# Mixer gates grouped by function over both halves, earlier load of x's second half, other column pacing and another end in a four-layer decoder trunk

## Chip, cores and metric

The kernel runs on one core of a Trainium2 chip. The metric is the device time of one execution in microseconds. Three runs of the kernel before took 1739.61, 1742.8 and 1742.51 us, median 1742.51.

## What is computed

x is (1024 positions, 1024 features), c one vector of 1024. Two blocks, each a token mixer and a squared-ReLU MLP, every one of the form x + gate(c) * f(RMSNorm(x) * (1 + scale(c)) + shift(c)), then a last RMSNorm. All values are float32. The reference, cut to what the change touches:

```python
cond = silu(c)
for i in range(2):
    mod = cond @ w_mod[i] + b_mod[i]                 # 6 x 1024 columns
    sh_m, sc_m, gt_m, sh_f, sc_f, gt_f = split(mod, 6)
    h = rms_norm(x, norm_mix_g[i]) * (1 + sc_m) + sh_m
    y = recurrent_mixer(h) if i == 0 else pool_mixer(h)
    x = x + gt_m * y
    h = rms_norm(x, norm_ffn_g[i]) * (1 + sc_f) + sh_f
    x = x + gt_f * (relu(h @ w1[i]) ** 2 @ w2[i])
return rms_norm(x, final_norm_g)

# recurrent_mixer
g = gelu(h @ w_y + b_y)
u = causal_conv4(h @ w_in + b_in)                    # width 4, per channel
r = sigmoid(u @ w_a + b_a); i = sigmoid(u @ w_x + b_x)   # 4 heads of 256 x 256
log_a = 8 * r * log_sigmoid(lam); a = exp(log_a)
s = scan: s_t = a_t * s_{t-1} + sqrt(1 - exp(2 log_a)) * i * u
return (s * g) @ w_out + b_out
```

## The kernel before

Features lie on the 128 partitions in 8 blocks, positions on the free axis in two halves of 512 (`x[0]`, `x[1]`). Every matrix product is split: a value v is kept as a high part of the TensorE type and a low rest, and `mm3` (L184) does three products, high by high, high by low, low by high, of 128x128 weights by 128x512. `proj` (L192) is 24 such products into one accumulator. There are 6 accumulators (`ps_mm`, L53), so a product group starts only when an earlier group was read out. Weights come as 512 KB units: `split_unit` (L168) loads one through SP's DMA queue into one of 3 raw buffers, copies the high part on ACT (L180) and subtracts the low part on DVE (L181), or on POOL, or with an accumulating DMA ("dma").

The modulation columns: `mod_column` (L205) is one DVE pass over a 512 KB piece of w_mod (`mb`, 128x1024) that multiplies by cond and sums. The first layer's scale and shift go another way (below); the other 10 vectors have 8 pieces each, 80 in all, in the order (0,2) (0,4) (0,3) (0,5) and then layer 1's. `drip(n)` (L229) does the next n of them; `split_unit` drips `rate[0]` or a given number after each load, `drip_until` (L233) does what is missing when a vector is needed. A piece takes one of the same 3 raw buffers and stands in DVE's order like any instruction.

The start: SP's queue gets vec, x's first half, and then in the order of the string at L113 the w_mod pieces `mw` 0 to 7 (digits; scale piece j=1, then shift piece j=0) and the four parts of the first projection's weights ("w"). `load_x(1)`, x's second half, comes at L409 behind two units of w_in. The loop at L380 does the first projection for half 0 (`ps6`, 18 products a block, L401) while scale and shift are still being computed. Its order on ACT, DVE and POOL is fixed by `after` (L321), which puts each instruction behind the one before on its engine: on DVE `bias_of(k)`, `scale_of(k+1)`, `hl` of block k, `normed(k+3)`. Squares of x's second half and their sums (`s1`, L443) follow behind the loop, then the copies `xr` that empty `ps6` (L426), two more projections, the scale `bc1` by the sums, the convolution (L431; four taps on ACT and DVE) and half 1.

The gates (L502) run per head and half: split of the head's input `xchl` (L507, L508), 8 groups of products of 6 products for two halves (4 per call), sigmoid of each, Exp and Tanh, a square on POOL (L529) and a multiply on DVE (L530), Sqrt (L533), products and the scan (L537). Behind each call two `gelu_block` (L542), each one `proj`, a gelu on ACT (L545) and a multiply on DVE. sigmoid, Exp and Tanh, Sqrt, and gelu need four different tables on ACT, and a load stands before each change. `split_y` (L550) splits the result for the output projection.

Elsewhere the order on each engine is made by a planner that takes the code's order as priority and its own estimate of when inputs are ready; `tc.issue_after` pins what is written in it.

After the output projection (L586, 8 drips in its first part), `ffn_norm` (L571) and 16 chunks of MLP follow (`f1`, `f2_fast`, `f2`), and the pooling mixer between them. `f1(0, 0)` (L858) has `ffn_norm(0, 1)` behind its first block, so PE does L272, the sums of x's half 1, there. `DRIPS` (L680) is one column for every unit of a chunk.

The end: `last_chunk` (L1013) does the last MLP product for half 0, for the first 256 positions of half 1 and for the rest. `SumSq` (L244) squares each new block of x on ACT and adds on DVE ("V") or opens a second part ("X"). The last norm uses `rstd_row` (L993), which sums over partitions with a 128x128 matrix of ones into 128x256 and takes root and reciprocal of that; the others use `rstd_bcast` (L265), which sums into 128x2 (one column per 128 positions), takes root and reciprocal there, and spreads with two more products.

Of the kernel before, what the change touches and what calls it, by code (L numbers as in the profile page):

```python
# [42 lines left out]
def trunk_kernel(ctx, tc, xT, vecs, wmod, w_k, w_in, w_y, w_g, w_out, w_p, w1, w2, outT):  # L43
# [69 lines left out]
    for what in "0ww1w2w34567":  # L113
        if what == "w":
            q = len(k_raw)
            if q == 0:
                kr = slot("kr")
            r2 = kr[:, q, :]
            r1 = slot("kr3", (D,)) if q == 3 else rawp.tile([P, D + 256], F32, tag="raw", name=f"raw_k{q}")[:, 0:D]
            k_raw.append((r1, r2))  # L120
            for part in range(2 if q == 0 else 1):
                for r, c0 in ((r1, 0), (r2, D)):
                    lo, hi = piece(r, q, part)
                    nc.sync.dma_start(r[:, lo:hi], w_k[q, :, c0 + lo:c0 + hi])
        else:
            e = int(what)
            for j in (1, 0):
                mod_raw[j, e] = mw[e][:, j, :]
                nc.sync.dma_start(mod_raw[j, e], wmod[0, j, e])
# [114 lines left out]
    class SumSq:  # L244


        def __init__(self, name, n=H, plan="GGGGGGGG", room=None):
            self.name, self.n, self.plan, self.room = name, n, plan, room
            self.parts = {}
            self.i = 0  # L250

# [12 lines left out]

    def rstd_bcast(ss, trace=None):  # L265
# [3 lines left out]
        ps = small_ps()  # L269
        for q in range(nq):  # L270
            for pi, a in enumerate(parts):
                PE.matmul(out=ps[:, q:q + 1], lhsT=a[:, q * P:(q + 1) * P], rhs=ones[:, 0:1],  # L272
                          start=(pi == 0), stop=(pi == len(parts) - 1))
# [99 lines left out]

    low = prepare(0)
# [5 lines left out]
    for k in range(NB):  # L380
# [15 lines left out]
        if k + 3 < NB:  # L396
            normed(k + 3)
        for low, r in ((0, hh), (0, hl), (1, hh)):
# [10 lines left out]
    load_x(1)  # L409
# [33 lines left out]
    s1 = SumSq("m01", plan="VVVVVVVV")  # L443
    for k in range(NB):
        s1.add(x[1][:, k, :])
# [56 lines left out]
    def gates(hd, unit, h):  # L502

        xchl = slot("xchl", (2, 2, H), F32R)
        xch, xcl = xchl[:, 0, :, :], xchl[:, 1, :, :]
        src = xc[h][:, 2 * hd:2 * hd + 2, :]
        S.copy(xch, src)  # L507
        V.tensor_sub(xcl, src, xch.bitcast(F32))  # L508
        rs, gs = [], []
        for mi in range(2):  # L510
            b = 2 * hd + mi
            for g in range(2):
                ps = acc_mm()
                for k in range(2):
                    mm3(ps, unit, ((g * 2 + k) * 2 + mi) * P, xch[:, k, :], xcl[:, k, :], k == 0, k == 1)
                t = tmp("gate")
                S.activation(t, ps, AF.Sigmoid, bias=vcol("ba" if g == 0 else "bx", b))
                (rs if g == 0 else gs).append(t)
        aa = []
        for mi in range(2):  # L520
            b = 2 * hd + mi

            av = tmp("a")
            S.activation(av, rs[mi], AF.Exp, scale=coef[:, b:b + 1])
            S.activation(rs[mi], rs[mi], AF.Tanh, scale=ncoef[:, b:b + 1])
            aa.append(av)
        for mi in range(2):
            e = tmp("asq")
            G.tensor_mul(e, aa[mi], aa[mi])  # L529
            V.scalar_tensor_tensor(rs[mi], e, 1.0, rs[mi], op0=ALU.add, op1=ALU.mult)  # L530
        for mi in range(2):
            b = 2 * hd + mi
            S.activation(rs[mi], rs[mi], AF.Sqrt)  # L533
            hs = xc[h][:, b, :]
            G.tensor_mul(gs[mi], gs[mi], hs)
            V.tensor_mul(gs[mi], gs[mi], rs[mi])
            V.tensor_tensor_scan(hs, aa[mi], gs[mi], 0.0 if h == 0 else carry[:, b:b + 1],  # L537
                                 op0=ALU.mult, op1=ALU.add)
            if h == 0:
                V.tensor_copy(carry[:, b:b + 1], hs[:, H - 1:H])  # L540
# [141 lines left out]
    def f1_jobs(i, c, eng=None):  # L682
        return [partial(lambda j: split_unit(w1[i, c * 4 + j], f"w1_{i}_{c}_{j}", eng, DRIPS[j]), j) for j in range(4)]
# [309 lines left out]
    def rstd_row(ss):  # L993

        parts = list(ss.parts.values())
        ps = small_ps()[:, 0:ss.n]
        for pi, a in enumerate(parts):
            PE.matmul(out=ps, lhsT=ones, rhs=a, start=(pi == 0), stop=(pi == len(parts) - 1))
        r = tmp("rrow", ss.n)
        S.activation(r, ps, AF.Sqrt, bias=eps, scale=1.0 / D)  # L1000
        V.reciprocal(r, r)
        return r

# [9 lines left out]
    def last_chunk(h, t0, n, plan, side=iter(())):  # L1013
        s = SumSq(f"o{h}{t0}", n, plan)
# [22 lines left out]
    sc = last_chunk(1, n1, H - n1, "VVVVVVVX", mid_norm())  # L1037
    final_norm(rstd_row(sc), 1, n1, H - n1)
# [71 lines left out]
```

## Time and profile before

| | us |
|---|---|
| median of 3 runs | 1742.51 |
| profiled execution | 1740.37 |
| its span, first to last instruction | 1738.5 |
| PE busy | 1690.5 (97%) |
| DVE busy | 1358.9 (78%) |
| ACT busy | 967.2 (56%) |
| POOL busy | 492.3 (28%) |
| DMA, mean | 108 GB/s; 340 GB/s in the first 60 us |

The profile is one execution. Times are in us from the span's start; PE is the TensorE matmul, PEld its weight load, DVE VectorE, ACT ScalarE, POOL GpSimd, SPq SyncE's DMA queue. In a timeline row the number in brackets is the engine's idle time before the instruction and who ended it. PE's mean granted clock is 0.994 of full.

The stages: first projection 0 to 58, the rest of w_in and the convolution to about 122, gates and gelu to about 250, output projection to about 359, then MLP and pooling, the last norm from 1700.

### The profile page before, as it was taken

The page shows a single profiled execution, that of the slowest core. Times are in us where ns is not written, and L with a number is a line of the kernel's source. Part 1 is how long each engine was busy: PE and PEld are TensorE (multiplying, and loading weights), DVE is VectorE, ACT ScalarE, POOL GpSimd, SP SyncE. Part 2 cuts the span into 40 slices and gives each one's busy share as a digit, 9 for nine tenths or more (in the row PEclk, how much of TensorE's full clock was granted, in tenths as well). Part 3 has the DMA queues.
Part 4 walks back from the last instruction along what each step waited for, and adds up shares of the span by engine and source line. Part 5 has one row for each costly group of instructions (what it writes and reads, how often), then busy time and mean ns, then how long its engine had stood idle before and what let it go on. Part 6 is the DMA issues. An engine that isn't in the chain of part 4 may idle for free.

```text
span 1738.5 us, 20871 instructions
## 1 busy us (share of the span) xinstructions
PE 1690.5 (97%) x7472; PEld 1386.7 (80%) x7472; DVE 1358.9 (78%) x2115; ACT 967.2 (56%) x1660; POOL 492.3 (28%) x419
## 2 busy tenths in 40 slices
PE   6899999999999999999999999999999999999997
PEld 4687778877788888888888888888878787878787
DVE  7897867589898989897973898559696868687847
ACT  6588886555454454545457787745444454545432
POOL 2132343103241414151416333303140405041403
PEclk9999999999999999999999999999999999999999
DMA  9423425642423333332319888841111112120202
GB/s 337 168 93 104 143 85 162 143 119 83 136 72 123 95 99 109 96 117 89 123 37 198 202 192 179 190 118 61 49 59 39 61 38 70 39 69 29 80 6 97
DMA packets 63175, 187.33 MB, mean 108 GB/s; under 512 B 6752, under 2 KB 9184, under 8 KB 63072
## 3 DMA queue, kind: packets, MB, share of 16 engines
q1 hardware_dynamic: 47376, 157.43, 27.6%
q0 software_dynamic: 15696, 28.58, 9.9%
q8 instruction: 58, 0.95, 0.2%
q14 instruction: 45, 0.37, 0.1%
HBM read 181.79 MB, written 4.19 MB: 107 GB/s over the span
## 4 chain that ended last, share of the span: by engine, by line
PE 75%; DVE 10%; issue 3%; ACT 3%; DMA 2%; POOL 1%; DVEq 0%; ACTq 0%; POOLq 0%
PE mm L188 25%; PE mm L189 25%; PE mm L190 25%; DMA mb<-in_wmod 2%; DVE mb L207 1%; DVE xa L773 1%; DVE xb L773 1%; POOL xa L782 1%; DVE xcb L440 1%; DVE w_a_s L181 1%; ACT c L777 0%; DVE gate L530 0%; PE sm L272 0%; DVE w_y L181 0%; DVE w_s L181 0%
## 5 line engine op out<-in xcount | busy, mean ns | idle before, releaser
L188 PE MATMUL mm<-hh,w_w 128*128 128x512 f32 x1024 | 399.7, 390 | 0.9 <-DVE xa L773 0.9
L189 PE MATMUL mm<-hl,w_w 128*128 128x512 f32 x1024 | 399.3, 390 | 0.0
L190 PE MATMUL mm<-hh,w_w 128*128 128x512 f32 x1024 | 399.0, 390 | 0.0
L782 POOL TENSOR_TENSOR xb<-xb,c 128x512 f32<-128x512 f32 x104 | 150.0, 1442 | 625.4 <-ACT c L777 625.2
L188 PEld LDWEIGHTS mm<-hh,w_w 128*128 128x128 f32 x1024 | 192.6, 188 | 43.1 <-DVE xa L773 3.0
L190 PEld LDWEIGHTS mm<-hh,w_w 128*128 128x128 f32 x1024 | 192.6, 188 | 40.2
L189 PEld LDWEIGHTS mm<-hl,w_w 128*128 128x128 f32 x1024 | 192.5, 188 | 39.5
L782 POOL TENSOR_TENSOR xa<-xa,c 128x512 f32<-128x512 f32 x104 | 159.7, 1535 | 145.2 <-ACT c L777 145.2
L777 ACT ACTIVATE c<-c,mod 128x512 f32<-128x512 f32 x104 | 75.3, 724 | 202.6 <-DVE c L803 135.5
L623 ACT ACTIVATE relu<-mm 128x512 f32<-128x512 f32 x128 | 76.2, 596 | 144.7 <-PE mm L190 144.7
L207 DVE SCALAR_TENSOR_TENSOR mb<-mb,cond 128x1024 f32<-128x1024 f32 x80 | 114.5, 1434 | 47.9 <-DMA mb<-in_wmod 47.9
L773 DVE SCALAR_TENSOR_TENSOR xa<-mm,mod,xa 128x512 f32<-128x512 f32 x156 | 113.0, 742 | 25.8 <-POOL xa L782 25.8
L181 DVE TENSOR_TENSOR w_w<-raw_w,w_w 128x512 fp32r<-128x512 f32 x112 | 106.8, 962 | 12.4 <-ACT w_w L180 12.4
L165 POOL DMA_DIRECT2D w_w<-in_w x80 | 70.5, 900 | 151.0 <-ACT w_w L164 120.6
L613 DVE TENSOR_TENSOR u<-usq,u 128x512 fp32r<-128x512 f32 x102 | 70.2, 688 | 16.1 <-ACT u L612 15.8
L188 PE MATMUL mm<-u,w_a_a 128*128 128x512 f32 x200 | 79.1, 396 | 2.3 <-DVE xb L773 1.2
L188 PE MATMUL mm<-u,w_w 128*128 128x512 f32 (+1 forms) x224 | 80.9, 361 | 0.0
L189 PE MATMUL mm<-u,w_w 128*128 128x512 f32 (+1 forms) x224 | 80.5, 360 | 0.1
L190 PE MATMUL mm<-u,w_w 128*128 128x512 f32 (+1 forms) x224 | 80.4, 359 | 0.0
L180 ACT CAST w_w<-raw_w 128x512 fp32r<-128x512 f32 x112 | 65.1, 612 | 25.0 <-PE mm L190 17.3
L189 PE MATMUL mm<-u,w_a_a 128*128 128x512 f32 x200 | 78.0, 390 | 0.0
L190 PE MATMUL mm<-u,w_a_a 128*128 128x512 f32 x200 | 77.9, 389 | 0.0
(326 smaller groups left out, 4030.0 us busy)
## 6 DMA issues: line engine op xcount, KB each, us to landing
raw_w<-in_w SPq DMA_DIRECT2D x148, 512.0 KB, 3.5
mb<-in_wmod SPq DMA_DIRECT2D x80, 512.0 KB, 3.8
w_w<-in_w POOLq DMA_DIRECT2D x80, 256.0 KB, 5.5
mw<-in_wmod SPq DMA_DIRECT2D x16, 512.0 KB, 11.0
raw_in<-in_w_in SPq DMA_DIRECT2D x8, 512.0 KB, 7.0
raw_y<-in_w_y SPq DMA_DIRECT2D x8, 512.0 KB, 3.7
raw_o<-in_w_out SPq DMA_DIRECT2D x8, 512.0 KB, 4.2
outT<-o SPq DMA_DIRECT2D x12, 256.0 KB, 2.2
```

What stands on the lines that cost most here:

```text
L165: nc.gpsimd.dma_start(w[:, 1, 0:n], src, accum_op=ALU.add)
L180: S.copy(w[:, 0, 0:n], raw)
L181: (eng or V).tensor_sub(w[:, 1, 0:n], raw, w[:, 0, 0:n].bitcast(F32))
L188: PE.matmul(out=ps, lhsT=wh, rhs=rh, start=first, stop=False)
L189: PE.matmul(out=ps, lhsT=wh, rhs=rl, start=False, stop=False)
L190: PE.matmul(out=ps, lhsT=w[:, 1, c:c + P], rhs=rh, start=False, stop=last)
L207: V.scalar_tensor_tensor(raw, raw, 1.0, cond, op0=ALU.mult, op1=ALU.mult, accum_out=m[:, e:e + 1])
L613: eng.tensor_sub(u[n][:, 1, jj, :], src, u[n][:, 0, jj, :].bitcast(F32))
L623: S.activation(r, ps, AF.Relu)
L773: V.scalar_tensor_tensor(xb, ps, g[:, r + 4 * row:r + 4 * row + 1], xb, op0=ALU.mult, op1=ALU.add)
L777: S.activation(t, src, AF.Identity, scale=g[:, r + 4 * row:r + 4 * row + 1])
L782: G.tensor_add(xb, xb, t)
```

## The change

Four places. x's second half is loaded between the w_mod pieces 5 and 6 (`345x67`), and its squares are done in the hand-ordered loop, three behind block 5, three behind 6, two behind 7 (`square1`). `gates` takes both halves: all sigmoids of both, then the split of the next head's inputs for both, then POOL's product of gate and input, Exp and Tanh of all four, the squares, the Sqrt; Exp writes over the convolution's output, and half 0's gates have a slot of their own. The four gelu blocks of a head follow, and `split_y(0)` stands behind the last head. The drip rate per unit is 0, 2, 3, 3 for the heads' units in place of 0, 1, 2, 3, and the first w1 units drip none. The last norm's sum is made on PE, one group of column sums for the first five blocks and one for each of the last three, and `rstd_bcast` replaces `rstd_row`.

```diff
-    for what in "0ww1w2w34567":
+    for what in "0ww1w2w345x67":
...
+        elif what == "x":
+            load_x(1)
...
+    class LastSumSq(SumSq):
+        def add(self, xb):
+            if self.i == 0:
+                self.ps = small_ps()
+            if self.plan[self.i] == "V":
+                super().add(xb)
+                if "V" in self.plan[self.i:]:
+                    return
+                a = self.parts["V"]
+            else:
+                a = tmp("sq", self.n)
+                self.i += 1
+                S.activation(a, xb, AF.Square)
+            for q in range(self.n // P):
+                PE.matmul(out=self.ps[:, q:q + 1], lhsT=a[:, q * P:(q + 1) * P], rhs=ones[:, 0:1],
+                          start=(a is self.parts["V"] and q == 0), stop=(self.i == NB), skip_group_check=True)
...
-        ps = small_ps()
...
+        ps = ss.ps
+        if ps is None:
+            ps = small_ps()
...
+    s1 = SumSq("m01")
+    def square1(k):
+        sq = tmp("sq")
+        after(S.activation, sq, x[1][:, k, :], AF.Square)
+        a = s1.parts.setdefault("V", sq)
+        if a is not sq:
+            after(V.tensor_add, a, a, sq)
...
+        for k1 in {5: (0, 1, 2), 6: (3, 4, 5), 7: (6, 7)}.get(k, ()):
+            square1(k1)
...
-    load_x(1)
...
-    s1 = SumSq("m01", plan="VVVVVVVV")
-    for k in range(NB):
-        s1.add(x[1][:, k, :])
...
-    def gates(hd, unit, h):
+    def gates(hd, unit, halves):
...
+        rs, gs = {}, {}
+        for h in halves:
+            xchl = split.pop((hd, h)) if (hd, h) in split else split_gate(hd, h)
+            room = slot("gates") if h == 0 else None
+            for mi in range(2):
+                b = 2 * hd + mi
+                for g in range(2):
+                    ps = acc_mm()
...
+                    t = tmp("gate") if room is None else room[:, 2 * mi + g, :]
+                    S.activation(t, ps, AF.Sigmoid, bias=vcol("ba" if g == 0 else "bx", b))
+                    (rs if g == 0 else gs)[h, mi] = t
+        if hd < 3:
+            for h in halves:
+                split[hd + 1, h] = split_gate(hd + 1, h)
+        both = [(h, mi) for h in halves for mi in range(2)]
+        hs = {(h, mi): xc[h][:, 2 * hd + mi, :] for h, mi in both}
+        for at in both:
+            G.tensor_mul(gs[at], gs[at], hs[at])
+        for at in both:
+            b = 2 * hd + at[1]
+            S.activation(hs[at], rs[at], AF.Exp, scale=coef[:, b:b + 1])
+            S.activation(rs[at], rs[at], AF.Tanh, scale=ncoef[:, b:b + 1])
+        for at in both:
             e = tmp("asq")
+            G.tensor_mul(e, hs[at], hs[at])
+            V.scalar_tensor_tensor(rs[at], e, 1.0, rs[at], op0=ALU.add, op1=ALU.mult)
+        for at in both:
+            h, b = at[0], 2 * hd + at[1]
+            S.activation(rs[at], rs[at], AF.Sqrt)
+            V.tensor_mul(gs[at], gs[at], rs[at])
+            V.tensor_tensor_scan(hs[at], hs[at], gs[at], 0.0 if h == 0 else carry[:, b:b + 1],
                                  op0=ALU.mult, op1=ALU.add)
...
-        rate[0] = hd
+        rate[0] = (0, 2, 3, 3)[hd]
...
+        gates(hd, ug, (0, 1))
         for h in range(2):
-            gates(hd, ug, h)
-            if (hd, h) == (3, 1):
-                split_y(0)
             for mi in range(2):
                 gelu_block(2 * hd + mi, uy[mi], h)
+    split_y(0)
...
-        return [partial(lambda j: split_unit(w1[i, c * 4 + j], f"w1_{i}_{c}_{j}", eng, DRIPS[j]), j) for j in range(4)]
+        return [partial(lambda j: split_unit(w1[i, c * 4 + j], f"w1_{i}_{c}_{j}", eng, 0 if (i, c) == (0, 0) else DRIPS[j]), j) for j in range(4)]
...
-    sc = last_chunk(1, n1, H - n1, "VVVVVVVX", mid_norm())
-    final_norm(rstd_row(sc), 1, n1, H - n1)
+    sc = last_chunk(1, n1, H - n1, "VVVVVXXX", mid_norm())
+    final_norm(rstd_bcast(sc), 1, n1, H - n1)
```

## Rows read from the trace of the kernel before

**Rows 1.** The page, busy time: engine, us, share of the span, instructions.
```profile
PE 1690.5 (97%) x7472; PEld 1386.7 (80%) x7472; DVE 1358.9 (78%) x2115; ACT 967.2 (56%) x1660; POOL 492.3 (28%) x419
```

**Rows 2.** PE's waits, whole span: line, releaser, us in total, times, longest.
```profile
PE mm L188 <- ACT gelu L545: 6.1, 4, 1.9
PE mm L188 <- ACT xr L426: 4.0, 1, 4.0
...
PE sm L272 <- DVE mod L210: 3.9, 1, 3.9
```

**Rows 3.** Timeline 42 to 79: start, us, engine, line, operation, idle before.
```profile
42.23 1.34 DVE L328 CUSTOM_DVE_ANT_0 mw<-mw,cond,bmix 128x1024 f32<-128x1024 f32 x1
42.35 0.81 ACT L328 ACTIVATE hh<-xn,mod,amix 128x512 fp32r<-128x512 f32 x1 [2.57 <-DVE mod L328]
...
46.75 1.07 PE L401 MATMUL mm<-hl,w_k 128*128 128x512 f32 x4
...
55.97 0.63 ACT L258 ACTIVATE ssqm01V<-xb 128x512 f32<-128x512 f32 x1 [1.42 <-DMA xb<-in_xT]
...
59.58 2.28 DVE L263 TENSOR_TENSOR ssqm01V<-ssqm01V,sq 128x512 f32<-128x512 f32 x3
...
61.11 3.56 ACT L426 ACTIVATE xr<-mm,vec 128x512 f32<-128x512 f32 x6
...
61.83 0.80 PE L188 MATMUL mm<-hh,w_in 128*128 128x512 f32 x1 [4.04 <-ACT xr L426]
...
67.12 0.48 PE L188 MATMUL mm<-hh,w_in 128*128 128x512 f32 x1
...
78.53 1.19 PE L188 MATMUL mm<-hh,w_in 128*128 128x512 f32 x4 [0.45 <-ACT hh L295]
```

**Rows 4.** The first raw_in on SP's queue: timeline row, then issue to landing.
```profile
31.64 0.33 SPq L99 DMA_DIRECT2D raw_in<-in_w_in  x1
...
raw_in<-in_w_in SPq DMA_DIRECT2D x1, 512.0 KB, 20.2
```

**Rows 5.** Gates: windows row (PE, PEld, DVE, ACT, POOL), groups (busy, mean | idle), timeline.
```profile
130.00:235.00 105.00, 98.88 (x432) 80.54 (x431) 86.52 (x122) 85.86 (x114) 33.94 (x23) 1.00 0.38 124
...
L207 DVE SCALAR_TENSOR_TENSOR mb<-mb,cond 128x1024 f32<-128x1024 f32 x17 | 25.2, 1489 | 10.7 <-DMA mb<-in_wmod 10.7
...
L524 ACT ACT_TABLE_LOAD x6 | 7.7, 1283 | 7.4 <-DVE coef L498 7.3
...
L533 ACT ACTIVATE gate<-gate 128x512 f32<-128x512 f32 x12 | 7.6, 633 | 12.1 <-DVE gate L530 12.0
...
234.57 0.62 PE L190 MATMUL mm<-hh,w_y 128*128 128x512 f32 x1
...
237.55 0.59 PE L188 MATMUL mm<-hh,w_y 128*128 128x512 f32 x1
```

**Rows 6.** Timeline 358 to 368, DVE and PE, behind the output projection.
```profile
358.83 1.23 DVE L207 SCALAR_TENSOR_TENSOR mb<-mb,cond 128x1024 f32<-128x1024 f32 x1 [2.08 <-DMA mb<-in_wmod]
...
361.26 1.23 DVE L207 SCALAR_TENSOR_TENSOR mb<-mb,cond 128x1024 f32<-128x1024 f32 x1 [0.59 <-DMA mb<-in_wmod]
...
363.24 1.02 PE L272 MATMUL sm<-ones,ssq 128*128 128x1 f32 x8 [3.94 <-DVE mod L210]
...
367.14 0.63 PE L286 MATMUL sm<-dg,ones_r 128*128 128x512 f32 x1
```

**Rows 7.** Timeline 1720 to 1732, the last two norms.
```profile
1720.30 0.50 PE L272 MATMUL sm<-ones,ssqo10V 128*128 128x1 f32 x4
...
1723.13 0.28 PE L286 MATMUL sm<-dg,ones_r 128*128 128x256 f32 x1
...
1727.41 0.47 DVE L832 SCALAR_TENSOR_TENSOR xb<-mm,mod,xb 128x256 f32<-128x256 f32 x1
...
1728.45 0.70 PE L998 MATMUL sm<-ssqo1256X,ones 128*128 128x256 f32 x2 [0.20 <-ACT ssqo1256X L258]
...
1731.48 3.26 DVE L1009 SCALAR_TENSOR_TENSOR o<-xb,vec,rrow 128x256 f32<-128x256 f32 x8
```

More of the change, by code (lines that the diff above doesn't have):

```diff
@@ L250, in __init__ @@
             self.i = 0
+            self.ps = None
         def add(self, xb):
@@ L268, in rstd_bcast @@
         parts = list(ss.parts.values())
-        ps = small_ps()
[L270 to L273, printed above, removed]
+        ps = ss.ps
+        if ps is None:
+            ps = small_ps()
+            for q in range(nq):
+                for pi, a in enumerate(parts):
+                    PE.matmul(out=ps[:, q:q + 1], lhsT=a[:, q * P:(q + 1) * P], rhs=ones[:, 0:1],
+                              start=(pi == 0), stop=(pi == len(parts) - 1))
         r = mp.tile([P, 4], F32, tag="rstd", name="rstd", bufs=2)
@@ L500, in trunk_kernel, with split_gate @@
     behind.close()
-    def gates(hd, unit, h):
+    def split_gate(hd, h):
         xchl = slot("xchl", (2, 2, H), F32R)
-        xch, xcl = xchl[:, 0, :, :], xchl[:, 1, :, :]
         src = xc[h][:, 2 * hd:2 * hd + 2, :]
[L507 to L527, printed above, removed]
-            e = tmp("asq")
[L529 to L537, printed above, removed]
@@ new lines, in split_gate @@
+        S.copy(xchl[:, 0, :, :], src)
+        V.tensor_sub(xchl[:, 1, :, :], src, xchl[:, 0, :, :].bitcast(F32))
+        return xchl
+    split = {}
+    def gates(hd, unit, halves):
[7 more added lines that the diff above has]
+                    ps = acc_mm()
+                    for k in range(2):
+                        mm3(ps, unit, ((g * 2 + k) * 2 + mi) * P, xchl[:, 0, k, :], xchl[:, 1, k, :], k == 0, k == 1)
+                    t = tmp("gate") if room is None else room[:, 2 * mi + g, :]
[13 more added lines that the diff above has]
+        for at in both:
+            e = tmp("asq")
+            G.tensor_mul(e, hs[at], hs[at])
[5 more added lines that the diff above has]
+            V.tensor_tensor_scan(hs[at], hs[at], gs[at], 0.0 if h == 0 else carry[:, b:b + 1],
@@ L538, in gates @@
                                  op0=ALU.mult, op1=ALU.add)
             if h == 0:
-                V.tensor_copy(carry[:, b:b + 1], hs[:, H - 1:H])
+                V.tensor_copy(carry[:, b:b + 1], hs[at][:, H - 1:H])
     def gelu_block(m, unit, h):
@@ L991, in trunk_kernel @@
     units = [split_unit(w2[1, 7, dp], f"w2_1_7_{dp}") for dp in range(4)]
[L993 to L1002, printed above, removed]
     def final_norm(bc, h, t0, n):
@@ L1013, in last_chunk @@
     def last_chunk(h, t0, n, plan, side=iter(())):
-        s = SumSq(f"o{h}{t0}", n, plan)
+        s = (LastSumSq if "X" in plan else SumSq)(f"o{h}{t0}", n, plan)
         for dp in range(4):
```

## The prediction, made before the change was run

> **What bounds the kernel now.** I read the page first: TensorE is busy 1690.5 of 1738.5 us [rows 1], so only the 48 us in which it idles, and the stretches in which its products run at half rate, can be won. The waits of PE say where they are: 6.1 us in four waits for the gelu on ACT, 4.0 in one for the copy xr on ACT, 3.9 in one for DVE [rows 2]. Then I read the time around each, engine by engine, because the engine that a wait names was itself late for something else.
>
> The wait for xr: ACT empties the accumulators only from 61.11 on, because the squares of x's second half stood ahead in its queue and waited for xb, whose first piece landed at 55.97. The next product starts at 61.83 after 4.04 us idle and is slow: from there to 67.12 the starts lie 0.43 us apart, not 0.23 (the lower of the clock's two levels, 1.2 GHz) [rows 3]. 12 products in 5.29 us are worth 12 x 0.229 = 2.7 us at full rate, so the stall costs 4.0 + 2.6 = 6.6 us.
>
> The gates: 98.88 us for 432 products is 0.229 us each, so the stage runs at full rate but for its waits. ACT loads a table for 1.28 us before each of sigmoid, Exp, Sqrt and gelu, for every head and half. Its 12 Sqrt wait 12.1 us in all, for DVE; the gelu stands behind it, and PE has no free accumulator until a gelu is done. DVE in turn stands 10.7 us in wait for the mb columns [rows 5]. After the last of these waits 8 products, those of 234.57 to 237.55, lie 0.43 apart: 8 x 0.2 = 1.6 us more.
>
> The third wait: DVE does an mb column at 358.83 after 2.08 us of waiting for its DMA, and another at 361.26. Between them stand the last adds to x's second half, so the sums that PE reads with L272 come at 363.24, 3.94 us late. Nine products behind it are slow as well, to about 367.6: 9 x 0.2 = 1.8 us [rows 6].
>
> **The change, part by part.**
>
> *x's second half.* Its four pieces go ahead of mw6 and mw7 in SP's queue: four 512 KB transfers change places with four. The queue lands in order, and the first raw_in, next behind mw7, lands at 31.64 + 20.2 = 51.8 [rows 4]. That is where mw6's scale half lands now; the next three follow up to 55.97. This adds a wait. scale_of(6) stood on DVE at 42.23 [rows 3], and the order written out by hand has hl of block 5 right behind it, so both wait until 51.8. PE needs that hl at 46.75 [rows 3]. From there DVE paces the stage, with 1.34 for a scale or a bias and 0.76 for an hl or an add [rows 3]: scale 53.1, hl 53.9, two adds of squares 55.4, bias of block 6 56.8, scale of block 7 58.1, hl of block 6, which needs two ACT passes of 0.81 behind the bias, 59.2, three adds 61.4, bias of block 7 62.8, hh 63.6, and 18 products at 0.229 on PE: 67.7. These products end at 57.8 now (61.83 less the 4.04). PE idles 7 us at 46.75; half rate behind it lies inside the chain and costs nothing more. The copy xr follows in 0.6 (3.56 for six [rows 3]), so the next projection starts at 68.3 at full rate. The old start at 61.83, with its 2.6 us lost to half rate, equals 64.4: a loss of 3.9. Some of it comes back: PE reaches the second half's first product at 78.53 [rows 3], though 48 products from 64.4 end at 75.4. The 3.1 between are waits for the scale of x's second half and its own small products. With the sums ready before the projection, I let half of it, 1.6, go. Taken: **-2.3**. Ends: +6.6 if mw6 lands as early as now, which the order of the queue speaks against; -3.9 if nothing comes back.
>
> *Gates for both halves.* Per head PE now does 8 groups of 6 products (48 x 0.229 = 11.0 us) and 4 gelu projections (96, 22.0): 33.0 us. ACT loads 4 tables, not 8: 16 loads fewer, 20.5 us. Counted from PE's first gate product: last sigmoid 11.7, table 13.0, eight Exp and Tanh at 0.73 (between a Sqrt's 0.63 [rows 5] and hh's 0.81 [rows 3]) 18.8, table and four Sqrt 22.6, table and the first gelu 24.6. With six accumulators, four of them held by gelus, PE waits only at the third group of the next head, at 33.0 + 2.7 = 35.7. That is 11.1 us in hand, against the 1.0 us that a Sqrt waits for DVE on average. So the four waits (6.1) and the slow stretch (1.6) go: 7.7. What is late next is DVE. The columns drip 0, 6, 9, 9 in place of 0, 3, 6, 9: six more here at 1.57 (1.49 and the 0.08 readout), 9.4 us, on an engine busy for 86.5 of 105 [rows 5]. The next head's split (two copies on ACT, two subtractions on DVE) is the old one at another place; PE needs it 20 us later. Head 0 has the least cover, because Exp already waits there for coef, which DVE computes behind the convolution; I take 1 us off. Taken: **+6.7**, ends 0 and 7.7.
>
> *Columns.* By the output projection 24 + 8 = 32 columns are through, all that the first layer needs: the four beside the first w1 units and the forced one go, and with them at least one of the two columns in the 3.94 us. The column of the first w2 unit stays. If it still lands as late, only the second column's 1.2 us is won; if neither is in the way, 3.9 + 1.8 = 5.7. The queue carries five 512 KB loads less ahead of it, so I take **+4.4**, near the upper end. The later chunks get their columns two earlier, beside products that PE does without these waits: 0, within 1 either way.
>
> *End.* Now: last x at 1727.41, the row sum on PE at 1728.45, the first output at 1731.48: 3.03. The other form stands in the trace for the first quarter: L272 at 1720.30, its second L286 over at 1723.41, with an add between, which at half the width of those in rows 3 I estimate at 0.4: 2.7 without it [rows 7]. Without the add that DVE does ahead of it, the last x can come up to 0.4 earlier too. Against these 0.7: each sum group is 0.50 on PE [rows 7], and two of the four fall ahead of the last product: -1.0. Taken: **0**, ends -0.7 and +0.7. The last 8 outputs and their DMAs stay.
>
> **Sum.** -2.3 + 6.7 + 4.4 + 0 = 8.8. The profiled execution took 1740.37 (span 1738.5 and 1.87 around it): 1731.6. The median shown, 1742.51, is 2.1 above it, the lowest of the three 0.8 below; I put the forecast 0.4 above the sum: **1732 us**. 0.2% (3.5 us) is about what a measurement of this kernel tells from no change.
>
> **The rivals.**
> *x's move eats the rest.* -3.9, half of the gates (3.5, since the late convolution keeps coef late in head 0) and 2 of the columns: 1.6 faster, 1739, which reads as no change. For it: DVE's order is fixed by hand and mw6 lands 9 us later. Against it: the gates alone hold 7.7.
> *The functions are not grouped.* The planner, not the code, orders ACT; a gelu whose accumulator is full may slip between Exp and Sqrt, and the loads stay. Then the gates give 0: 1738. Against it: now no gelu stands ahead of a Sqrt, though ACT waits there.
> *Slower: DVE becomes the bound of the gates.* Busy 86.5 + 9.4 = 96 us. Its waits in order: 10.7 us for 17 columns [rows 5], so 14.5 for 23, and some 4 for POOL and ACT. If none of these are filled, the stage takes 115 us in place of 105. It decides from the point where DVE's lag exceeds the 11.1 us in hand, which two heads of 9 columns, entered late by x's move, could just reach. Price: 10 longer, x -3.9, columns +5.7: 8.2 slower, 1749. Against it: units are split a head ahead, and the last head has no columns, so a lag can drain.
> The Trainium skill (SBUF — State Buffer, "SBUF: two separate sides") says that a POOL operation and a DVE operation with two SBUF inputs shut each other out for a whole instruction. POOL is busy 33.9 us beside DVE's 86.5 in 105 us [rows 5]: together 120, so the lock cannot hold for all of them, but a column's mean of 1.49 here against 1.23 in rows 6 agrees with it in part. By the rule in full the stage would be 86.5 + 33.9 + 9.4 = 130 us, 25 longer; I count it inside this rival.
>
> **How the numbers follow.** Forecast 0.60, x's move 0.15, not grouped 0.10, DVE as bound 0.15. The forecast's own range, from its ends (x -3.9 to 0, gates 5 to 7.7, columns 1.2 to 5.7, end -0.7 to 0.7), is 2 to 14 faster, mostly 1726 to 1737. The range of 8 in 10 takes in both cases of no change and leaves out the deeper half of the slower one: 1725 to 1744. Faster by over 0.2%: the forecast and the better part of the ungrouped case, 0.65; within 0.2% 0.20; slower 0.15.
>
> **What would show it.** x: PE idle about 7 us near 47 with DVE waiting for mw, the wait for xr gone, the second half's first product near 80. Gates: 16 table loads fewer, no wait of PE for gelu, 33 us a head; wrong if a wait for gelu, xchl or w_g stands there. Columns: L272 of the output projection's second half waits under 1.5 us. End: from the last x to the first output under 3 us. The prediction is wrong if PE's idle between 40 and 60 exceeds 11 us, or if DVE is busy over 95% through two heads and PE waits behind it.

## The result and the profile after

After: median 1760.76 us (1757.54 to 1762.58), before beside it 1741.06 (1739.43 to 1742.8); ratio 1.0111, 95% interval 1.0091 to 1.0131. The change made the kernel 1.1% slower; the forecast had it 0.6% faster. The profiled execution's span is 1758.1 us, 19.6 longer than before's. Three marks on PE, read from the timelines, say where they went:

| first product of | before | after | later by |
|---|---|---|---|
| the gates (w_g) | 122.76 | 130.22 | 7.5 |
| the output projection (w_o) | 262.26 | 279.58 | 17.3 |
| the first layer's second matrix (w_a_a) | 401.41 | 420.61 | 19.2 |
| the span's end | 1738.5 | 1758.1 | 19.6 |

So 7.5 us are lost ahead of the gates, where of the four places only x's has changed, 9.9 in the gates, 1.9 in the output projection and behind it, 0.4 after that. (In the runs below whose start is that of the kernel before, the first mark lies between 122.06 and 123.67, so a difference of one microsecond in it says nothing.) PE's waits of after, whole span (line, releaser, us in total, times, longest), to be read beside [rows 2]:

```profile
PE mm L436 <- DVE hl L352: 8.2, 2, 7.9
...
PE sm L310 <- DVE dg L308: 5.2, 3, 2.3
PE mm L191 <- DVE xchl L538: 5.1, 1, 5.1
...
PE mm L190 <- ACT w_g L182: 4.5, 1, 4.5
...
PE mm L192 <- POOL w_o L183: 3.0, 1, 3.0
PE mm L190 <- ACT hh L319: 2.8, 1, 2.8
```

All three waits of [rows 2] are gone, as forecast. In their place stand waits for things that are prepared ahead: hl in the first projection, the split xchl of a head's input, the splits w_g and w_o of weights. x's stage in the timelines of DVE and PE, against [rows 3]:

```profile
52.55 1.34 DVE L352 CUSTOM_DVE_ANT_0 mw<-mw,cond,bmix 128x1024 f32<-128x1024 f32 x1 [9.73 <-DMA mw<-in_wmod]
...
54.56 2.07 PE L436 MATMUL mm<-hl,w_k 128*128 128x512 f32 x4 [7.93 <-DVE hl L352]
...
68.25 0.95 PE L296 MATMUL sm<-ones,sq 128*128 128x1 f32 x8
...
83.51 2.08 PE L190 MATMUL mm<-hh,w_in 128*128 128x512 f32 x4 [2.78 <-ACT hh L319]
```

The gates: the windows row over the same 105 us as in [rows 5] (busy of PE, PEld, DVE, ACT, POOL, then PE's granted clock), and the five groups of table loads from 125 to 285 (busy, mean ns | idle before):

```profile
130.00:235.00 105.00, 98.06 (x422) 80.05 (x421) 85.19 (x115) 84.29 (x109) 38.78 (x24) 0.97 0.41 131
```
```profile
L560 ACT ACT_TABLE_LOAD x8 | 10.3, 1283 | 0.1
L572 ACT ACT_TABLE_LOAD x8 | 10.3, 1283 | 0.1
L580 ACT ACT_TABLE_LOAD x8 | 10.3, 1283 | 0.1
L573 ACT ACT_TABLE_LOAD x4 | 5.1, 1283 | 0.1
L590 ACT ACT_TABLE_LOAD x4 | 5.1, 1283 | 0.1
```

32 loads, not 16. Per head the table of sigmoid (L560) is loaded twice, that of Exp and Tanh (L572, L573) three times, that of Sqrt (L580) twice, and only gelu's (L590) once, because an Exp stands between sigmoids and a Tanh between Sqrt. DVE is busy 85.2 us of 105, not more than before. Head 0, on three engines (ACT, DVE, PE):

```profile
135.37 1.05 ACT L537 CAST xchl<-xcb 128x1024 fp32r<-128x1024 f32 x1
...
142.69 1.22 DVE L538 TENSOR_TENSOR xchl<-xcb,xchl 128x1024 fp32r<-128x1024 f32 x1
...
143.96 0.79 PE L191 MATMUL mm<-xchl,w_g 128*128 128x512 f32 x1 [5.15 <-DVE xchl L538]
```

The split of half 1's input is copied on ACT behind three sigmoids, 5.15 us after the first gate product. From the copy's end at 136.42 to the subtraction on DVE another 6.3 us pass, in which DVE does the low part of a w_g unit, three taps of the convolution and two columns. The same copy in the kernel before, on ACT:

```profile
114.57 1.05 ACT L507 CAST xchl<-xcb 128x1024 fp32r<-128x1024 f32 x1
```

There it ran 8.2 us ahead of that product. Head 3 in after, on SP's queue, ACT and PE:

```profile
210.94 0.33 SPq L99 DMA_DIRECT2D raw_g<-in_w_g  x1
...
214.62 0.62 ACT L182 CAST w_g<-raw_g 128x512 fp32r<-128x512 f32 x1 [5.07 <-DMA raw_g<-in_w_g]
...
243.15 0.62 ACT L182 CAST w_g<-raw_g 128x512 fp32r<-128x512 f32 x1
...
243.82 0.79 PE L190 MATMUL mm<-xchl,w_g 128*128 128x512 f32 x1 [4.48 <-ACT w_g L182]
```

The first copy of w_g stands on ACT ahead of a sigmoid and waits 5.07 us for its load; the second comes 28.5 us later, behind the gelus. The columns, on DVE and PE, against [rows 6]:

```profile
382.92 1.23 DVE L209 SCALAR_TENSOR_TENSOR mb<-mb,cond 128x1024 f32<-128x1024 f32 x1 [2.44 <-DMA mb<-in_wmod]
...
384.88 0.50 PE L310 MATMUL sm<-dg,ones_r 128*128 128x512 f32 x1 [2.25 <-DVE dg L308]
```

The sums L296 (L272 before) no longer wait; the column of the first w2 unit now stands right behind them on DVE. And the end on DVE, against [rows 7], last x and first output:

```profile
1747.17 0.48 DVE L876 SCALAR_TENSOR_TENSOR xb<-mm,mod,xb 128x256 f32<-128x256 f32 x1 [1.61 <-PE mm L192]
...
1751.06 3.22 DVE L1042 SCALAR_TENSOR_TENSOR o<-xb,vec,sm 128x256 f32<-128x256 f32 x8 [0.68 <-PE sm L310]
```

3.89 us from the start of the one to the start of the other, where it was 4.07 (1727.41 to 1731.48 in [rows 7]). The prediction's 3.03 counts from the row sum on PE at 1728.45; from the last sum on PE, at 1748.21, it is 2.85 here.

### The profile page after: what moved, and what is told of

Its sections match the earlier page's. It is cut to its first block, busy times and chain, and to the rows that moved or that the text cites. A ratio compares the mean times of both kernels' runs of the same rounds, so it can differ in the third digit from the quotient of the medians.

```text
span 1758.1 us, 20887 instructions
## 1 busy us (share of the span) xinstructions
PE 1697.3 (97%) x7486; PEld 1392.1 (79%) x7486; DVE 1359.4 (77%) x2117; ACT 968.5 (55%) x1660; POOL 503.5 (29%) x419
## 4 chain that ended last, share of the span: by engine, by line
PE 75%; DVE 9%; issue 3%; ACT 3%; DMA 2%; POOL 1%; DVEq 0%; ACTq 0%; POOLq 0%
PE mm L190 25%; PE mm L192 25%; PE mm L191 25%; DMA mb<-in_wmod 2%; DVE xa L817 1%; DVE xb L817 1%; DVE mb L209 1%; POOL xa L826 1%; DVE w_a_s L183 1%; DVE w_s L183 1%; ACT c L821 0%; DVE raw_w L772 0%; DVE c L847 0%; DVE xcb L474 0%; PE sm L296 0%
```

## The experiments

Ratios are to the kernel before, run beside each; w_g and w_o are the two marks above.

| run | ratio, 95% interval | w_g | w_o |
|---|---|---|---|
| x_alone | 1.0029, 1.0017 to 1.0040 | 128.84 | 265.66 |
| gates_alone | 1.0102, 1.0086 to 1.0117 | 122.71 | 268.96 |
| columns_alone | 1.0037, 1.0025 to 1.0050 | 122.19 | 270.94 |
| end_alone | 1.0008, 0.9999 to 1.0016 | 122.25 | 261.14 |
| gates_split_first | 1.0053, 1.0041 to 1.0066 | 122.77 | 261.36 |
| grouped | 1.0073, 1.0060 to 1.0086 | 122.78 | 274.80 |
| grouped_split_first | 1.0034, 1.0022 to 1.0045 | 122.29 | 267.43 |
| room_only | 1.0202, 1.0188 to 1.0216 | 122.45 | 296.26 |
| after_no_x | 1.0092, 1.0079 to 1.0106 | 122.38 | 275.79 |
| after_no_columns | 1.0133, 1.0119 to 1.0147 | 129.24 | 274.38 |
| grouped_wo | 0.9974, 0.9964 to 0.9983 | 122.99 | 258.27 |
| grouped_no_cols_last | 0.9993, 0.9984 to 1.0002 | 123.67 | 254.23 |
| split_first_wo | 1.0033, 1.0021 to 1.0046 | 122.06 | 259.72 |
| grouped_wo_cols | 1.0011, 1.0002 to 1.0020 | 122.27 | 267.90 |
| x_behind | 1.0027, 1.0018 to 1.0036 | 129.09 | 267.29 |
| moved_cols | 0.9957, 0.9945 to 0.9970 | 122.44 | 256.88 |
| moved_cols24 | 0.9987, 0.9978 to 0.9996 | 122.75 | 263.10 |

**Each part alone.** The four edits of the change, one at a time on the kernel before. x_alone:

> The kernel before with only the load and the squares of x's second half changed. The trace of after had its first gate product 7.4 us later than before (130.2 against 122.8). Theory (each part costs where it stands): the move alone delays the first gate product by 6 to 8 us and the whole by as much, ratio 1.0035 to 1.0055; PE waits 7 to 8 us near 54 for hl L345-equivalent and then 2 to 3 us for hh of the second half. Rival (the sum of the prediction, -2.3): ratio about 1.0015. Rival (the late convolution also costs a wait in head 0, 5.1 us in after at 143.96): ratio 1.006 to 1.008.

gates_alone:

> The kernel before with only the gates of both halves, the early split of the next head and the place of the second split; columns at the old rate 0, 1, 2, 3 and x as before. The order of ACT still loads a table 32 times. Theory (the joint call itself costs: loads stay, unit splits with later place in the code come late): 2 to 6 us slower, ratio 1.001 to 1.0035, with a wait of PE for w_g of head 3. Rival (the gates suffer in after only from the late convolution and from the added columns): 3 to 7 us faster, ratio 0.996 to 0.998, no PE wait over 1.5 us between the first gate product and the output projection.

columns_alone:

> The kernel before with only the column rates (0, 2, 3, 3) and none beside the first w1 units. Theory (the columns cost in the gates what they give back later): gates 2 to 5 us later, the wait of 3.9 us for the sums at the end of the output projection gone, together 0 to 2 us either way, ratio 0.999 to 1.001. Rival (prediction): 4.4 us faster, ratio 0.9975. Rival (the added columns are what holds up the units of head 3 and of the output projection): slower by 3 to 6 us, ratio 1.002 to 1.0035.

end_alone:

> The kernel before with only the last norm's sum changed. Prediction and theory: no change, within 0.7 us, ratio 0.9996 to 1.0004; the time from the last x to the first output within 0.7 of 3.03 us. No rival expects over 1 us.

All four are slower or equal, and together (1.76%) they exceed the whole (1.11%), so some overlap. The gates are the large one, and larger than my expectation allowed: 17.8 us, with the convolution as early as before and no added columns. x costs 5.0 us, a little under the expected 6 to 8; head 0 did not wait in it. The columns miss the theory and the prediction and come near the third expectation (1.0037 against 1.002 to 1.0035): the wait of 3.9 us went, but the output projection begins 8.7 us later. The end's ratio, 1.0008, lies above the expected 1.0004, with an interval that holds 1.

Most of what the columns cost is one chain over three engines. In columns_alone, on DVE, ACT and PE:

```profile
234.23 1.23 DVE L207 SCALAR_TENSOR_TENSOR mb<-mb,cond 128x1024 f32<-128x1024 f32 x1 [2.94 <-DMA mb<-in_wmod]
...
236.10 0.63 ACT L533 ACTIVATE gate<-gate 128x512 f32<-128x512 f32 x1 [4.75 <-DVE gate L530]
...
241.01 0.79 PE L188 MATMUL mm<-hh,w_y 128*128 128x512 f32 x1 [5.62 <-ACT gelu L545]
```

A column waits on DVE for its load; the multiply L530 stands behind it, the Sqrt on ACT waits for that multiply, the gelu stands behind the Sqrt, and PE waits for an accumulator until the gelu is done. PE's waits for gelu are 12.4 us in all, where they were 6.1.

**What holds up the split.** In gates_alone PE waited 1.12 and 6.04 us for xchl in head 0. Of the 19 slots, 16 hold x, the convolution's output, hh and hl of both halves; three are left. Before, three splits rotate through them. The change gives one to half 0's gates. room_only gives it to the kernel before and changes nothing else:

```diff
         rs, gs = [], []
+        room = slot("gates") if h == 0 else None
...
-                t = tmp("gate")
+                t = tmp("gate") if room is None else room[:, 2 * mi + g, :]
```

> The kernel before with one edit: half 0's sigmoids go into a slot of their own, as after the change, and not into four small buffers; gates are called half by half as before. In the order on ACT an Exp then comes between sigmoids and a Tanh between Sqrt in half 0, and the split of half 1 goes behind a gelu. Theory (the slot by itself holds the splits up and lets the functions interleave): 4 to 12 us slower, ratio 1.0025 to 1.007. Rival (the slot is harmless, the joint call is what costs): within 2 us, ratio 0.999 to 1.001.

35 us slower, three times the upper end of what was expected: the slot alone is enough. Head 0 in room_only on ACT and PE:

```profile
129.41 0.73 ACT L525 ACTIVATE a<-gates,coef 128x512 f32<-128x512 f32 x1
130.15 1.28 ACT L518 ACT_TABLE_LOAD   x1
131.44 0.69 ACT L518 ACTIVATE gates<-mm,vec 128x512 f32<-128x512 f32 x1
...
144.78 1.04 ACT L507 CAST xchl<-xcb 128x1024 fp32r<-128x1024 f32 x1
...
145.86 2.07 PE L188 MATMUL mm<-xchl,w_g 128*128 128x512 f32 x4 [6.93 <-ACT xchl L507]
```

The split of half 1 moved from 114.57 to 144.78, behind a gelu, and PE waited for such a split six times (its waits row):

```profile
PE mm L188 <- ACT xchl L507: 27.5, 6, 6.9
```

Exp (L525) stands between sigmoids (L518) too, as in after; why the planner mixes them with the slot and not with the small buffers was not tried.

gates_split_first takes the slot later than head 0's splits, with gates_alone otherwise the same:

```diff
+    split.update({(0, h): split_gate(0, h) for h in range(2)})
     for hd in range(4):
```

> The gates alone, as in the run before (ratio 1.0102), but the splits of head 0's input for both halves stand in the code ahead of the first head, so ahead of the slot that half 0's gates take; the order on ACT then has the split of half 1 six instructions before the end of the convolution, as in the kernel before, and not behind three sigmoids. Theory (the new slot, not the convolution, held the split up): the PE waits of 1.12 and 6.04 us for xchl in head 0 go, with 2 to 3 us of half rate behind them: 8 to 10 us of the 17.8, ratio 1.0045 to 1.006. Rival (DVE is late with the convolution, whatever the order): the wait stays above 4 us, ratio 1.008 to 1.011.

The theory held: 8.5 us of the 17.8 went. The copy on ACT in this run is back at its old place, and heads 0 to 2 take 32.64 us each with no wait of PE. The loss that is left arises in the last head and the output projection, in waits of PE of 1.75 us for a gelu, 3.89 for a sigmoid, 0.93 for yl (the low part that `split_y` makes on DVE) and 4.63 for w_o on POOL. The copy:

```profile
114.44 1.05 ACT L506 CAST xchl<-xcb 128x1024 fp32r<-128x1024 f32 x1 [1.78 <-DVE xcb L440]
```

**Grouping the functions.** On gates_alone, ACT's order is pinned, so that a table is loaded 4 times a head:

```diff
+    def order_s():
+        return tc.issue_after(tail_s[0].ins) if tail_s[0] is not None else nullcontext()
...
-            S.activation(rs[at], rs[at], AF.Sqrt)
+            with order_s():
+                root = S.activation(rs[at], rs[at], AF.Sqrt)
...
+        tail_s[0] = root
```

(The same is done for sigmoid, Exp, Tanh and gelu, each kind behind the last of the kind before.)

> The gates alone, with ACT's order pinned so that a head's Exp and Tanh come behind its last sigmoid, its Sqrt behind the last Tanh, its gelu behind the last Sqrt and the next head's sigmoids behind the last gelu: 16 table loads in place of 32. Theory (in gates alone PE waits for the split of head 0 and for weights of the last head and of the output projection, not for functions): head 0's wait of 6 us stays, 0 to 5 us of the 17.8 go, ratio 1.0075 to 1.010. Rival (my forecast fell because the functions were not grouped; 16 loads fewer free 20.5 us of ACT): ratio at or under 1.002, unit splits no longer late.

With head 0's splits first as well:

> Both: head 0's splits ahead of the slot, and ACT's order pinned. Theory (the two add; only the wait for w_o on POOL in the output projection, 4.6 us, stays): ratio 1.000 to 1.004. Rival (with both gone the joint gates do what was forecast, 6.7 us faster): 0.996 to 0.998. Rival (PE still waits at half rate behind other splits): 1.006 or more.

The first lies just past the good end of its theory (1.0073 against 1.0075; 5.0 us less than gates_alone). The second lies within its theory, except that the wait for w_o on POOL is gone and another stands in head 3. On SP's queue, ACT and PE of grouped_split_first:

```profile
216.20 16.12 SPq L222 DMA_DIRECT2D mb<-in_wmod  x3
233.14 8.88 SPq L99 DMA_DIRECT2D raw_o<-in_w_out  x4
```
```profile
238.01 0.62 ACT L180 CAST w_o<-raw_o 128x512 fp32r<-128x512 f32 x1 [9.60 <-DMA raw_o<-in_w_out]
238.54 0.68 ACT L571 ACTIVATE gelu<-mm,vec 128x512 f32<-128x512 f32 x1
```
```profile
239.27 0.80 PE L188 MATMUL mm<-xchl,w_g 128*128 128x512 f32 x1 [7.51 <-ACT gelu L571]
```

A chain from SP's queue over ACT to PE: three columns take 16 us to get raw buffers, raw_o is issued behind them, its copy stands on ACT one place ahead of head 2's last gelu, and PE, with no free accumulator for head 3's gates, waits for that gelu.

**Taking the copy of w_o from there, by order or by fewer columns.** grouped_wo pins it behind the last head's Tanh; grouped_no_cols_last leaves the nine columns of the last head out of the gates:

```diff
+    with tc.issue_after(tanh_of[0].ins):
-    wo = [split_unit(w_out[m], f"o{m}", G, 0) for m in range(4)]
+        wo = [split_unit(w_out[m], f"o{m}", G, 0) for m in range(4)]
```
```diff
-        rate[0] = hd
+        rate[0] = (0, 1, 2, 0)[hd]
```

> The gates with head 0's splits first and ACT's order pinned (1.0034), and the first weights of the output projection pinned behind the last head's Tanh on ACT. In the trace of the run without this pin a copy of w_o stood ahead of the last gelu of head 2 and waited 9.6 us for its DMA; PE lost 7.5 and 2.7 us and then ran at half rate. Theory (the place of that copy in ACT's order is the last cost): 9 to 13 us less, ratio 0.9965 to 0.9985. Rival (the columns hold the raw buffers, so the output projection waits for w_o instead): 1.000 to 1.003 with a PE wait for w_o of 4 us or more.

> As the run with splits first and pinned order (1.0034), with no columns beside the last head's units (rates 0, 1, 2, 0): nine columns fewer by the output projection, seven of which are forced in one go at the next norm. Theory (it is the nine columns that keep the raw buffers from w_o, so that its copy on ACT waits): the waits for gelu of 7.5 and 2.7 us fall under 2 us in all and the first product of the output projection comes 8 to 11 us earlier (256 to 259); what the forced columns cost later is open, ratio 0.997 to 1.003. Rival (the order alone): the waits stay above 6 us.

Both remove the 7.5 us, so the copy's place and the columns are two handles on one chain; grouped_wo, as its theory had it, is faster than the kernel before (by 0.26%, with an interval that leaves out 1). In grouped_no_cols_last a head takes 32.64 us each (w_g at 123.67, 156.31, 188.95, 221.59) with no wait of PE in any: the forecast's 33.0 us a head. What it wins there is lost again behind it: w_o comes at 254.23, 4.0 us before grouped_wo's, but PE waits 3.70 us at 328.81 for the sums behind the forced columns, and the first w_a_a product comes at 400.79, 2.45 us after grouped_wo's.

split_first_wo has both fixes and 32 table loads:

> The joint gates with head 0's splits first and w_o pinned behind the last head's Tanh, but ACT's order otherwise left to the planner: 32 table loads, as after. The same with pinned order and 16 loads stands at 0.9974. Theory (ACT has some 11 us in hand a head, so 16 loads of 1.28 us are hidden; only the order of splits and w_o cost): 0.9965 to 0.9985, no PE wait for ACT in the gates over 3 us. Rival (grouping itself is worth the 0.002 to 0.003 that it gave in the two earlier pairs, 1.0102 to 1.0073 and 1.0053 to 1.0034): 0.999 to 1.001.

Neither came as put: 1.0033 is slower than both. In heads 0 to 2 the loads are hidden: w_g at 122.06, 154.70, 187.34 and 219.98, 32.64 us a head with 32 loads as with 16. The last head has no gates behind it, and there ACT is late with w_o (PE's timeline):

```profile
259.72 0.80 PE L188 MATMUL mm<-yh,w_o 128*128 128x512 f32 x1 [4.53 <-ACT w_o L180]
...
264.68 0.80 PE L190 MATMUL mm<-yh,w_o 128*128 128x512 f32 x1 [3.74 <-POOL w_o L181]
```

With head 0's splits first, all four combinations of grouping and the pin of w_o were run:

| | 32 loads | 16 loads, ACT's order pinned |
|---|---|---|
| w_o not pinned | 1.0053 | 1.0034 |
| w_o pinned | 1.0033 | 0.9974 |

Each is worth 0.002 alone and 0.006 beside the other. So neither the loads nor the place of the copies costs the whole, and what grouping adds beside the pin lies behind the third head: 6.0 of the 7.5 us between split_first_wo's first w_a_a product (405.83) and grouped_wo's (398.34) arise after the first w_o. Pinning ACT's order changes the number of loads and the order at once; the two weren't tried apart.

**x.** x_behind loads x's second half behind all w_mod pieces (`34567x`) on the kernel before, with the squares in the loop as after:

> The kernel before with x's second half loaded behind all w_mod pieces (34567x), ahead of the first w_in unit, and its squares in the loop as after. Theory (x's price, 8 us of PE wait for hl in the first projection, comes from pieces 6 and 7 landing late): that wait goes, the first gate product comes within 3 us of 122.8 in place of 128.8, ratio 0.9990 to 1.0015. Rival (the squares in the loop, which wait for x on ACT ahead of the next block's hh, cost as much): 1.002 to 1.004 with a PE wait for hh of 4 us or more.

The rival came true (1.0027). ACT and PE of x_behind:

```profile
51.78 1.15 ACT L330 ACTIVATE sq<-xb 128x512 f32<-128x512 f32 x2 [6.99 <-DMA xb<-in_xT]
...
56.05 0.81 ACT L330 ACTIVATE hh<-xn,mod,amix 128x512 fp32r<-128x512 f32 x1 [1.96 <-DVE mod L330]
```
```profile
56.92 2.07 PE L414 MATMUL mm<-hh,w_k 128*128 128x512 f32 x4 [6.63 <-ACT hh L330]
```

The wait for hl is gone and one for hh, 6.63 us, stands in its place: the squares wait for x until 51.78 on ACT, and the next hh, and DVE's bias for it, stand behind them. In after it was mw6 that DVE waited for until 52.55. In these two runs the loop's hand order puts a block behind whichever of the two comes second, and the place in the queue chooses which. x loaded early with its squares left behind the loop was not run.

**What the parts cost together.** after_no_x is after with x undone, after_no_columns with the rates and the first w1 units undone.

> The kernel after with x's second half loaded and squared as before. After stands at 1.0111; its parts alone at 1.0029 (x), 1.0102 (gates), 1.0037 (columns), 1.0008 (end), together 1.0176. Theory (x's cost lies ahead of the gates and is added whole, so the overlap is between gates and columns): 1.0065 to 1.0085, and head 0 still waits 5 us or more for the split of half 1. Rival (the late convolution overlaps with the gates' own wait): 1.010 to 1.012.

> The kernel after with the old column rates 0, 1, 2, 3 and the old columns beside the first w1 units. Theory (columns and gates overlap: both hold up the units of the last head through the raw buffers): 1.010 to 1.0125. Rival (columns add what they cost alone): 1.0065 to 1.0085.

The first lies between the two expectations, the second above both. x is worth some 0.002 within after (the intervals overlap), less than alone: with the gates 7.8 us earlier, head 0's wait grows from 5.15 to 8.28 us, since the split on DVE comes only 3.9 us earlier (138.76 against 142.69). And the columns, a loss alone, are a gain of 0.0022 within after (3.8 us). By the marks they still cost 4.2 us in the gates (from w_g to w_o 149.4 us with them, 145.1 without; alone they cost 9.25 there), where without them a wait of 3.66 us for a sigmoid on ACT stands. But they win 7.7 us from w_o to the first w_a_a product (141.0 against 148.8; alone 0.8): without them PE waits there 0.74 us for yl, 4.65 for w_o and 4.23 for the sums, with them 2.96 for w_o and 2.25 behind the sums.

**The columns where the gates have slack.**

> The version at 0.9974 (splits first, pinned order, pinned w_o) with the columns of after: rates 0, 2, 3, 3 and none beside the first w1 units. Theory (with the gates in slack the columns cost little there and give back the 3.9 us wait at the end of the output projection less the 2.3 to 2.8 that the w2 unit's column still costs): 0 to 3 us faster than without, ratio 0.9955 to 0.9975. Rival (six more columns keep raw buffers and DVE in the heads, as alone, 8.7 us in the gates): 0.9995 to 1.002, with PE waits for gelu or w_y over 4 us.

The rival came true: 0.0037 slower than grouped_wo, as much as the columns cost alone. The chain of above stands a head earlier, with w_g for w_o; on SP's queue and ACT of this run:

```profile
184.74 15.84 SPq L222 DMA_DIRECT2D mb<-in_wmod  x3
201.40 0.33 SPq L99 DMA_DIRECT2D raw_g<-in_w_g  x1
```
```profile
205.69 0.62 ACT L180 CAST w_g<-raw_g 128x512 fp32r<-128x512 f32 x1 [9.02 <-DMA raw_g<-in_w_g]
206.22 0.68 ACT L571 ACTIVATE gelu<-mm,vec 128x512 f32<-128x512 f32 x1
```

moved_cols and moved_cols24 leave no column between the second w_y and the next w_g; the first with 18 columns in the heads as before, the second with 24 (4 and 4) and none beside the first w1 units:

```diff
-        rate[0] = hd
-        ug = split_unit(w_g[hd], f"g{hd}")
-        uy = [split_unit(w_y[m], f"y{m}") for m in (2 * hd, 2 * hd + 1)]
+        ug = split_unit(w_g[hd], f"g{hd}", None, 3 * (hd > 0))
+        uy = [split_unit(w_y[2 * hd + j], f"y{2 * hd + j}", None, (3, 0)[j] * (hd > 0)) for j in range(2)]
```

> The version at 0.9974 with its 18 columns of the heads set otherwise: three behind w_g and three behind the first w_y of heads 1 to 3, none behind the second w_y, so that the next head's w_g follows it in SP's queue. Theory (the place of the columns, not their number, sets the wait): the 2.8 us wait for gelu goes, 2 to 4 us faster than without, ratio 0.9950 to 0.9970. Rival (the number of columns on DVE): the same as before, 0.997 to 0.998. Rival (w_y is now late behind six columns): 0.999 or more with a PE wait for w_y.

> The same with four and four columns, 24 in the heads as after, and none beside the first w1 units; the same 24 at rates 0, 2, 3, 3 stood at 1.0011 with PE waits for gelu of 6.9 and 3.6 us. Theory (place): these waits fall under 3 us in all and the 3.9 us at the end of the output projection become 2 to 2.5, ratio 0.9940 to 0.9970. Rival (number): waits over 6 us in the gates stay, ratio 1.000 to 1.002.

moved_cols is the fastest version, 0.43% under the kernel before (7 us by the medians, 1734.21 against 1741.32); PE's wait for gelu in it is 1.9 us in all, less than the 2.8 of grouped_wo but not gone, and its interval overlaps with grouped_wo's. With 24 columns the waits fall from 10.5 to 6.4 us and the ratio from 1.0011 to 0.9987, between the ranges of theory and rival, with intervals that do not meet: the place counts. So does the number: 0.9987 with 24 against 0.9957 with 18. The wait for the sums at the output projection's end still stands in moved_cols, with 4.3 us.

## Why the prediction was wrong

The measured 1760.8 us lie beyond the forecast's range (to 1744) and beyond its slowest rival (1749). Below, each part has its forecast and its ends in us, faster positive, and then what it measured alone by its ratio.

*x: forecast -2.3, lower end -3.9; alone -5.0.* The mechanism was right to within a microsecond: the scale came at 52.55, PE idled 7.9 us, and the next projection's products started at 69.06, behind 0.8 us of sums, against 68.3. The step that failed is "Some of it comes back": instead of the 3.1 us of waits that I saw vanish, one of 2.78 us for the second half's first hh took their place, at 83.51 where I had put "near 80". Behind it PE ran at half rate, a term that the sum does not have at this place: 2.5 of the 7.5 us at the first gate product arise there (last section). Nor is mw6 the only cause, as x_behind shows.

*Gates: forecast +6.7, ends 0 and 7.7; alone -17.8.* This is the main error, and two steps failed. The first is "The next head's split ... is the old one at another place; PE needs it 20 us later". It took head 0's own split of half 1 as ready, because before it was; I had read the new slot in the code and gave it no cost. room_only and gates_split_first show that cost: 35 us for the slot on the kernel before, and 8.5 of the 17.8 us back when head 0's splits take their slots first. The other is "units are split a head ahead": a unit's copy is split in time only while its load is issued in time and the copy's place on ACT lets nothing important wait behind it. The 11.1 us in hand counted ACT's functions alone; the copies of splits and weights stand in the same order and were put at nothing, and one of them held PE up for 7.51 us in grouped_split_first. The sign that was named for this part came: waits for xchl and w_g. The 33 us a head were right (32.64 in heads 0 to 2 of six runs), and were reached with either order of the functions. "ACT loads 4 tables, not 8" was wrong and cost nothing in heads 0 to 2; the rival that had it named the right fact with the wrong price.

*Columns: forecast +4.4, ends 1.2 and 5.7; alone -6.4.* The wait at the end went, and the w2 unit's column took back 2.25 of the 3.94 us in after. What failed is where the six added columns were priced: 9.4 us of DVE beside work with slack. Their price is what stands behind them: alone, a column's wait for its load on DVE ahead of the gates' multiply (5.62 us of PE's time in columns_alone); with the gates grouped, three raw buffers held ahead of the next unit's load (6.94 us in grouped_wo_cols). Within after they are worth +3.8 in all.

*End: forecast 0, ends -0.7 and +0.7; alone -1.4, with an interval that holds 0.* From the last x to the first output it is 3.70 us in end_alone against 4.07, so the shorter form won 0.4, where 0.3 was forecast. The stretch ahead of it, which has two of the sum groups in it, grew by more than the 1.0 that was taken for them: from the third-last x to the last it is 4.71 us (1725.00 to 1729.71) where it was 3.37 (1724.04 to 1727.41). Together that is -1.0 in the traces, just past the lower end. The sign "from the last x to the first output under 3 us" mixed two starting points, since that time was 4.07 before.

*The rivals.* Slower came true, by another mechanism than "DVE becomes the bound": DVE is busy 85.2 of 105 us, not over 95%, though head 0's wait ends with an instruction of DVE. The rule of the Trainium skill (SBUF — State Buffer, "SBUF: two separate sides"), that a DVE operation with two SBUF inputs and a POOL operation that reads SBUF shut each other out for a whole instruction, is not refuted by the prediction's sum of 120 us in 105, nor by 85.2 + 38.8 = 124 here. Rows of after agree with it in part: the subtraction for w_g at 135.37, beside a POOL product from 134.99 to 136.58, took 1.76 us, the one at 132.82, with POOL idle, 0.69. The longer time counts as busy, so busy times of the two engines can add up to more than the span either way.

## What to carry to other kernels

Before a function gets a buffer from a pool, count who rotates through it: a buffer that holds results may be the one that let the next inputs be prepared early, and the loss shows up in the wait for those inputs. On an engine that runs in order, an instruction that waits for a DMA costs whatever stands behind it; look for loads that share their buffers with background transfers, and put these where no load follows that is needed soon. Work that an engine saves (here 16 loads) is worth its time only where that engine ends last: nothing in heads 0 to 2. And two fixes on one chain can each look small until both are in (grouping and the pin of w_o: 0.002 each alone, 0.008 together).

## What the runs showed of the hardware

The stalls cost more than their length, because PE is slow for a while behind them. Windows rows of grouped_split_first, around and behind the wait of 7.51 us at 239.27 (busy of the engines, then PE's granted clock):

```profile
233.00:262.00 29.00, 22.73 (x91) 18.56 (x92) 19.55 (x24) 23.87 (x37) 15.69 (x11) 0.82 0.27 90
262.00:290.00 28.00, 28.00 (x125) 23.21 (x124) 22.53 (x31) 11.18 (x20) 14.42 (x5) 1.00 0.40 125
```

91 products at the 0.229 us of [rows 5] are 20.8 us; the 29 us hold these, 6.3 us of idle time and 1.9 of slow products. The same behind x's wait of 2.78 us, from the second half's first product to the first gate product, in after and then in before:

```profile
83.51:130.22 46.71, 46.71 (x193) 38.08 (x193) 46.46 (x80) 32.95 (x52) 15.18 (x6) 0.93 0.22 69
```
```profile
78.53:122.76 44.23, 44.19 (x193) 35.99 (x193) 44.10 (x72) 33.85 (x54) 10.66 (x6) 1.00 0.20 64
```

193 products take 2.5 us longer in after, and its granted clock is 0.50, the lower level, from 83.51 to 89.50 and 1.00 from there on. The first 30 us are no part of this: there the clock differs between profiled executions whose start is the same code (1.00 in before, 0.77 in moved_cols).
